# Differential-attention layer: keys stored as two parts in DRAM, their high part read twice

## The chip, the cores and the metric

The kernel runs on one core of a Trainium2 chip. The metric is the device time of one execution in microseconds (us). The core has a matrix engine (PE, TensorE), whose granted clock the profile shows, a vector engine (DVE), a scalar engine (ACT), GpSimd (POOL), and SyncE (SP), which in this kernel issues every transfer (DMA).

## The reference, cut to what matters

One layer of a hybrid encoder is run for 2048 prompt rows and for 64 sample rows that see a cache of 1024 earlier keys. The change touches the product of queries and keys alone:

```python
proj = x @ p['w_in']
q, k, v, u = jnp.split(proj, [ATTN_WIDTH, 2 * ATTN_WIDTH, 3 * ATTN_WIDTH], axis=-1)
q = partial_rope(q.reshape(bsz, seq, 2 * N_HEADS, HALF_DIM), pos)
k = partial_rope(k.reshape(bsz, seq, 2 * N_HEADS, HALF_DIM), pos)
...
s = jnp.einsum('bqhd,bkhd->bhqk', q, k).astype(jnp.float32) * (HALF_DIM ** -0.5)
s = jnp.where(mask[None, None], s, -jnp.inf)
a = jax.nn.softmax(s, axis=-1)
w = (a[:, :, 0] - lam * a[:, :, 1]).astype(v.dtype)
o = jnp.einsum('bhqk,bkhd->bqhd', w, v).astype(jnp.float32)
```

There are 16 maps (8 heads of two), each with 32 dimensions for q and k. The rest of the layer is a state-space branch with a gated unit, an output projection, two layer norms and a feed-forward block of width 4096.

## The kernel before, in words

**High and low parts.** A float32 operand of a product is split into a high part in a shorter format and the low part that is left (`split`, line 127: ACT or another engine rounds, line 130 or 132; DVE or POOL subtracts, line 133). A product then takes three terms: high by high, high by low, low by high. For most products these are three matmuls (`mm3`, lines 136 to 138). For queries and keys a map has only 32 dimensions, so the three terms are stacked along the contraction: 3 x 32 = 96 rows in one matmul (line 515), and 99 with three rows of mask for the causal blocks (line 517).

**Writing queries and keys.** `proj_qk` (line 337) runs over 17 blocks of 128 rows. For each it makes q and k (lines 367 to 371), rotates them, and one block later `pend` calls `transposes` (line 346) once for q and once for k: four PE transposes, a split into the tiles tph (high) and tpl (low), and then the writes to DRAM. The scratch tensors have three slots per dimension (lines 216 to 219). Queries are written as high, low, high: slots 0 and 2 get tph, slot 1 gets tpl. Keys are written as high, high, low: slots 0 and 1 get tph, slot 2 gets tpl. That makes three writes for q and three for k in each block; a write has runs of 128 columns (64 for the sample's keys). `cache_keys` (line 394) does the same for the cached keys, eight tiles of 128 x 512, each written three times to KC (lines 413 to 415).

**Reading them.** `load_maps` (line 444) loads what one head needs: for each of two maps a query tile (tag q, three buffers) and one or two key tiles of up to 1024 columns (tag k, five buffers). A query tile is two transfers: 96 rows of QS, where the dimension and the slot of [512, 3, columns] merge into one row index (line 450), and three mask rows (line 451). A key tile is likewise two: 96 rows (line 456) and three mask rows (line 457). The first matmul of a unit that reads a tile waits for all its transfers. Heads are run in four sets of query blocks (line 1332), 8 heads each, and the third set also has a sample unit per head, which reads KC in tiles of 1024 and 64 columns.

**The order of the work.** All transfers stand in one queue, that of SP, in the order which the build gives them. The build orders the instructions of each engine by a model of their times and by priorities (`schedule_with_timeline_sim`, line 1470; `tc.high_priority`), so the order in one engine's queue isn't that of the source. In the projection of q and k (lines 1276 to 1281) the state-space branch is woven in between; in the attention (lines 1331 to 1368) the gated unit, the output projection and the feed-forward block are. A load of weights (tiles raw) or of a map waits in SP's queue until its buffer is free, and all that stands behind it waits too.

Of the kernel before, what the change touches and what calls it, by code (L numbers as in the profile page):

```python
# [13 lines left out]
F32R = mybir.dt.float32r  # L14
# [8 lines left out]
SEQ = 2048  # L23
DEC = 64
PAST = 1024
NT = SEQ + 2 * DEC
NL = NT // 128
AW = 512
# [85 lines left out]
def build(nc, tc, io, ctx):  # L114
# [8 lines left out]
    def dma(out, in_):  # L123
        f = lambda a: a.bitcast(F32) if a.dtype == F32R else a
        sync.dma_start(out=f(out), in_=f(in_))

    def split(dst_hi, dst_lo, src, hi_eng=None, lo_eng=None):

        if (hi_eng or act) is act:
            act.activation(out=dst_hi, in_=src, func=AF.Copy)  # L130
        else:
            hi_eng.tensor_copy(out=dst_hi, in_=src)  # L132
        (lo_eng or dve).tensor_tensor(out=dst_lo, in0=src, in1=dst_hi.bitcast(F32), op=ALU.subtract)  # L133
# [6 lines left out]
    def tt(e, out, a, b, op):  # L140
        e.tensor_tensor(out=out, in0=a, in1=b, op=op)  # L141
# [70 lines left out]
    def scratch(name, shape, dt=F32):  # L212
        return dr.tile(shape, dt, name=name)


    QS = scratch("s_q", [AW, 3, NT], F32R)
    KS = scratch("s_k", [AW, 3, SEQ], F32R)
    KC = scratch("s_kc", [AW, 3, PAST + DEC], F32R)
    QPARTS, KPARTS = ((0, 2), (1,)), ((0, 1), (2,))
    VS = scratch("s_v", [NH, 128, NL, 2, HD], F32R)  # L220
    VC = scratch("s_vc", [NH, 128, PAST // 128, 2, HD], F32R)
    KMS, QMS = (scratch("s_" + n, [3, 1024], F32R) for n in ("km", "qm"))
# [33 lines left out]
    def load_x(xp, b):  # L256

        n = 256 if b < 8 else 128
        h = xp.tile([128, 8, 256], F32R, tag="xh", name="xh")
        l = xp.tile([128, 8, 256], F32R, tag="xl", name="xl")  # L260
        for q in range(4):
            raw = xp.tile([128, 2, 256], F32, tag="xr", name="xr")
            dma(out=raw[:, :, :n], in_=io["xT"][q * 256:(q + 1) * 256, b * 256:b * 256 + n].rearrange("(k p) n -> p k n", p=128))
            split(h[:, 2 * q:2 * q + 2, :n], l[:, 2 * q:2 * q + 2, :n], raw[:, :, :n], lo_eng=XLO[(b + q) % len(XLO)])
        return h, l
# [71 lines left out]
    def proj_qk(wq, wk, xp, x0, c2):  # L337

        op = c2.enter_context(tc.tile_pool(name="o1", bufs=2, side="right"))
        pm = c2.enter_context(tc.tile_pool(name="pm1", bufs=QB, space=PSUM, side="right"))  # L340
        pt = c2.enter_context(tc.tile_pool(name="pt1", bufs=2, space=PSUM, side="right"))
        cs = op.tile([128, 2, NL, 8], F32, name="cs", bufs=1)
        dma(out=cs[:, 0], in_=io["cos8"])
        dma(out=cs[:, 1], in_=io["sin8"])

        def transposes(src, dst, parts, ncol, c0):
            ps = pt.tile([128, 4, 128], F32, tag="pt", name="pt")
            for c in range(4):
                pe.transpose(out=ps[:, c, :], in_=src[:, c * 128:(c + 1) * 128], identity=ident)
            h = op.tile([128, 4, 128], F32R, tag="tph", name="tph")  # L350
            l = op.tile([128, 4, 128], F32R, tag="tpl", name="tpl")
            split(h, l, ps)
            for t_, js in zip((h, l), parts):
                for j in js:
                    dma(out=dst.rearrange("(c p) j n -> p c j n", p=128)[:, :, j, c0:c0 + ncol], in_=t_[:, :, :ncol])

        xs = [x0]
        pend = None
        for i in range(NL):
            if i % 2 == 0:  # L360
                xh, xl = xs.pop(0)
                if i + 2 < NL:
                    xs.append(load_x(xp, i // 2 + 1))
            ts_ = slice(i % 2 * 128, i % 2 * 128 + 128)
            nrow = 128 if i < 16 else 64
            qk = op.tile([128, 1024], F32, tag="qk", name="qk")
            for cg, (wh, wl) in ((1, wk), (0, wq)):
                ps = pm.tile([128, 512], F32, tag="pm", name="pm")
                for kk in range(8):
                    mm3(ps, xh[:, kk, ts_], xl[:, kk, ts_], wh[:, kk], wl[:, kk], kk == 0, kk == 7)  # L370
                act.activation(out=qk[:, cg * 512:cg * 512 + 512], in_=ps, func=AF.Copy, scale=(SM_SCALE, 1.0)[cg])
            x8 = qk.rearrange("p (m d) -> p m d", d=32)[:, :, 0:8]
            ra = op.tile([128, 32, 8], F32, tag="ra", name="ra", bufs=1)
            rb = op.tile([128, 32, 8], F32, tag="rb", name="rb", bufs=1)
            tt(dve, ra, x8, cs[:, 0, i:i + 1, :].to_broadcast([128, 32, 8]), ALU.mult)
            tt(dve, rb[:, :, 0:4], x8[:, :, 4:8], cs[:, 1, i:i + 1, 0:4].to_broadcast([128, 32, 4]), ALU.mult)
            tt(dve, rb[:, :, 4:8], x8[:, :, 0:4], cs[:, 1, i:i + 1, 4:8].to_broadcast([128, 32, 4]), ALU.mult)
            tt(dve, x8, ra, rb, ALU.add)
            r0 = i * 128
            dma(out=io["k_o"][r0:r0 + nrow, :], in_=qk[:nrow, 512:1024])  # L380
            if pend:
                pend()

            def pend(qk=qk, i=i, r0=r0):
                transposes(qk[:, 0:512], QS, QPARTS, 128, r0)
                if i < 16:
                    transposes(qk[:, 512:1024], KS, KPARTS, 128, r0)
                else:
                    transposes(qk[:, 512:1024], KC, KPARTS, 64, PAST)
            yield  # L390
        pend()
        yield

    def cache_keys(c2):
        op = c2.enter_context(tc.tile_pool(name="ck", bufs=CKB, side="right"))
        for i in range(PAST // 128):
            raw = op.tile([128, 512], F32, tag="ckr", name="cvr")
            dma(out=raw, in_=io["cv"][i * 128:i * 128 + 128, :])
            for q, t_ in enumerate("hl"):
                vv = op.tile([128, 4, 2, HD], F32R, tag="ck" + t_, name="cvv")  # L400
                split_v(vv, raw[:, q * 256:q * 256 + 256])
                dma(out=VC.rearrange("h p i e d -> p i h (e d)")[:, i, q * 4:q * 4 + 4], in_=vv.rearrange("p h e d -> p h (e d)"))
            if i % 2:
                yield
        for c in range(4):
            for hf in range(2):
                h = op.tile([128, 512], F32R, tag="ckh", name="ckh")
                l = op.tile([128, 512], F32R, tag="ckl", name="ckl")
                rr, cc = slice(c * 128, (c + 1) * 128), slice(hf * 512, hf * 512 + 512)
                raw = op.tile([128, 512], F32, tag="ckr", name="ckr")  # L410
                dma(out=raw, in_=io["ckT"][rr, cc])
                split(h, l, raw, hi_eng=pool, lo_eng=pool)
                for t_, js in zip((h, l), KPARTS):
                    for j in js:
                        dma(out=KC[rr, j, cc], in_=t_)
                yield


# [25 lines left out]
    def load_maps(a, h, ksrc, nk, q0, nq):  # L444

        kt, qt = [], []
        for m in range(2):
            r = slice((2 * h + m) * 32, (2 * h + m) * 32 + 32)
            qt.append(a.qp.tile([KROWS, 512], F32R, tag="q", name="qst"))
            dma(out=qt[m][0:96, :nq], in_=QS[r, :, q0:q0 + nq].rearrange("r j n -> (r j) n"))  # L450
            dma(out=qt[m][96:KROWS, :nq], in_=QMS[:, :nq])
            kt.append([])
            for c0 in range(0, nk, 1024):
                n = min(nk - c0, 1024)
                t = a.kp.tile([KROWS, 1024], F32R, tag="k", name="kst") if n > 64 else a.k2.tile([KROWS, 64], F32R, tag="k%d" % m, name="ks2")
                dma(out=t[0:96, :n], in_=ksrc[r, :, c0:c0 + n].rearrange("r j n -> (r j) n"))
                dma(out=t[96:KROWS, :n], in_=KMS[:, :n])
                kt[m].append(t)
        return kt, qt
# [163 lines left out]
    def head_units(a, h, j0, j1):  # L623
        got = []

        def head():
            if not got:
                nk = j1 * 256
                kst, qst = load_maps(a, h, KS, nk, j0 * 256, nk - j0 * 256)
                vt = [a.vp.tile([128, 8, 128], F32R, tag="v", name="vt") for c in range(0, 2 * j1, 8)]  # L630
# [7 lines left out]
    def sample_unit(a, h):  # L638
        got = []

        def head():
            if not got:
                kst, qst = load_maps(a, h, KC, PAST + DEC, SEQ, DEC)
                vt = [a.vp.tile([128, 8, 128], F32R, tag="v", name="vt"), a.k2.tile([128, 1, 128], F32R, tag="v", name="vt2")]
# [715 lines left out]
    with cw:  # L1360
# [13 lines left out]
        with ExitStack() as c2:  # L1374
# [3 lines left out]
            b, l = B[3], B[2]  # L1378
# [23 lines left out]
            t = third()  # L1402
# [82 lines left out]
```

## Time and profile before

| what | value |
|---|---|
| median of 2 runs | 3099.81 us (3096.27 and 3103.34) |
| the profiled execution: its own time | 3108.33 us |
| its span, first to last instruction | 3106.6 us |
| PE busy | 2878.8 us (93% of the span) |
| DVE, ACT, POOL busy | 1768.3, 1501.3, 1646.6 us |
| mean granted clock of PE | 0.955 of full speed |
| bytes moved | 424.41 MB, of them 93.64 MB written to DRAM |

The rows below come from the profiled execution; a busy time of PE counts matmuls in flight, and the granted clock is a share of full speed. The share of DMA is the mean busy share of the core's 16 transfer engines. Transfers that SP issues have no busy time on SP itself; a row of SPq gives how long the issuing instruction stood in SP's sequencer.

### The profile page before, as it was taken

The numbers are of one execution on the slowest core, as the hardware profiler recorded it, in microseconds if no ns is written. First come the engines' busy times: TensorE is split into PE (matmuls) and PEld (weight loads), VectorE is DVE, ScalarE is ACT, GpSimd is POOL, SyncE is SP. The second block draws the span as 40 slices with busy tenths as digits, with TensorE's granted clock in tenths as the row PEclk, the third lists the DMA queues.
The fourth block names the chain that finished last, engine by engine and source line by source line (L and its number), as shares of the span: only waits on it lengthen the run. The fifth ranks groups of instructions, "written<-read, shape, count | busy, mean of one in ns | idle before, by whom it ended". The sixth has DMA issues, their size and how long they took to land.

```text
span 3106.6 us, 46392 instructions
## 1 busy us (share of the span) xinstructions
PE 2878.8 (93%) x15648; PEld 2415.2 (78%) x15648; DVE 1768.3 (57%) x4631; ACT 1501.3 (48%) x2905; POOL 1646.6 (53%) x1552
## 2 busy tenths in 40 slices
PE   8998999698989999999789999998799999989996
PEld 7976666598778888887578888876588888868885
DVE  7126776568787655658687666666526222442124
ACT  4222222677676666766566766752323333323332
POOL 2227752255665656656555666654545444555554
PEclk9999999699889999999889999999899999999998
DMA  6369774756744444446633333337322222253332
GB/s 190 114 202 229 211 193 125 219 156 188 224 131 127 144 120 125 128 133 196 186 110 111 107 107 111 94 112 264 98 83 68 79 82 82 82 170 94 99 99 71
DMA packets 419618, 424.41 MB, mean 137 GB/s; under 512 B 53394, under 2 KB 312978, under 8 KB 418356
## 3 DMA queue, kind: packets, MB, share of 16 engines
q1 hardware_dynamic: 419380, 421.46, 46.0%
q8 instruction: 123, 2.02, 0.3%
q14 instruction: 115, 0.94, 0.1%
HBM read 327.71 MB, written 93.64 MB: 136 GB/s over the span
## 4 chain that ended last, share of the span: by engine, by line
PE 64%; DVE 12%; DMA 11%; POOL 4%; issue 4%; ACT 3%; SPq 1%; DVEq 0%; POOLq 0%; ACTq 0%
PE pu L138 7%; PE pu L136 7%; PE pd L136 7%; PE pu L137 7%; PE pd L138 7%; PE pd L137 7%; PE oT L578 3%; PE tps L562 3%; PE sps L515 3%; DVE acc L141 2%; DMA raw<-in_ln_g 2%; DVE s L518 2%; POOL dl L133 1%; POOL s L141 1%; PE pm L138 1%
## 5 line engine op out<-in xcount | busy, mean ns | idle before, releaser
L133 POOL TENSOR_TENSOR dl<-raw,dh 128x512 fp32r<-128x512 f32 x336 | 438.5, 1316 | 328.0 <-ACT dh L130 294.0
L133 POOL TENSOR_TENSOR fwl<-raw,fwh 128x512 fp32r<-128x512 f32 x256 | 332.6, 1303 | 327.5 <-ACT fwh L130 288.6
L141 POOL TENSOR_TENSOR s<-s 128x512 f32<-128x512 f32 (+3 forms) x344 | 382.3, 1136 | 227.3 <-ACT s L546 209.3
L518 DVE TENSOR_SCALAR_CACHE_REDUCE s<-sps 128x512 f32<-128x512 f32 (+5 forms) x688 | 400.1, 599 | 169.8 <-PE sps L515 94.7
L136 PE MATMUL pu<-bxh,fwh 128*128 128x256 f32 (+2 forms) x1472 | 488.8, 334 | 3.5 <-ACT fwh L130 1.5
L137 PE MATMUL pu<-bxl,fwh 128*128 128x256 f32 (+2 forms) x1472 | 484.9, 331 | 0.0
L138 PE MATMUL pu<-bxh,fwl 128*128 128x256 f32 (+2 forms) x1472 | 482.1, 331 | 1.0 <-POOL fwl L133 0.9
L136 PE MATMUL pd<-dh,hh 128*128 128x512 f32 (+1 forms) x1088 | 430.3, 401 | 23.2 <-DVE acc L1025 8.6
L137 PE MATMUL pd<-dl,hh 128*128 128x512 f32 (+1 forms) x1088 | 429.8, 396 | 0.0
L138 PE MATMUL pd<-dh,hl 128*128 128x512 f32 (+1 forms) x1088 | 417.3, 397 | 3.8 <-POOL hl L133 2.0
L526 ACT ACTIVATE s<-s,nm 128x1024 f32<-128x1024 f32 (+9 forms) x416 | 365.6, 881 | 112.9 <-DVE nm L523 105.1
L130 ACT ACTIVATE dh<-raw 128x512 fp32r<-128x512 f32 x336 | 209.0, 628 | 390.5 <-PE pd L138 152.7
L141 DVE TENSOR_TENSOR acc<-acc,pd 128x512 f32<-128x512 f32 (+1 forms) x384 | 252.8, 681 | 241.9 <-PE pd L138 239.5
L132 DVE CAST hh<-fr 128x256 fp32r<-128x256 f32 (+2 forms) x184 | 106.2, 577 | 375.6 <-ACT fr L1178 375.4
L136 PEld LDWEIGHTS pu<-bxh,fwh 128*128 128x128 f32 x1472 | 279.3, 190 | 33.2 <-ACT fr L1177 3.0
L130 ACT ACTIVATE fwh<-raw 128x512 fp32r<-128x512 f32 x256 | 160.5, 628 | 295.5 <-DMA raw<-in_w_up 149.4
L137 PEld LDWEIGHTS pu<-bxl,fwh 128*128 128x128 f32 x1472 | 279.1, 190 | 25.4
L138 PEld LDWEIGHTS pu<-bxh,fwl 128*128 128x128 f32 x1472 | 276.5, 189 | 27.5 <-POOL fwl L133 2.6
L578 PE MATMUL oT<-w,vt 128*128 128x256 f32 (+3 forms) x1296 | 251.3, 295 | 14.2 <-DVE w L133 9.4
L136 PEld LDWEIGHTS pd<-dh,hh 128*128 128x128 f32 (+1 forms) x1088 | 202.3, 186 | 68.1 <-DVE hh L132 9.9
L515 PE MATMUL sps<-kst,qst 96*128 96x512 f32 (+2 forms) x544 | 219.6, 422 | 35.5 <-DVE s L518 28.7
L578 PEld LDWEIGHTS oT<-w,vt 128*128 128x128 f32 (+1 forms) x1296 | 206.2, 196 | 43.9 <-DVE w L133 16.3
(273 smaller groups left out, 5921.4 us busy)
## 6 DMA issues: line engine op xcount, KB each, us to landing
raw<-in_w_up SPq DMA_DIRECT2D x256, 256.0 KB
raw<-in_w_down SPq DMA_DIRECT2D x256, 256.0 KB
kst<-s_k SPq DMA_DIRECT2D x64, 384.0 KB
raw<-in_w_out SPq DMA_DIRECT2D x80, 256.0 KB
xr<-in_xT SPq DMA_DIRECT2D x64, 256.0 KB
vt<-s_v SPq DMA_DIRECT2D x32, 512.0 KB
qst<-s_q SPq DMA_DIRECT2D x64, 192.0 KB
s_q<-tph SPq DMA_DIRECT2D x34, 256.0 KB
```

The costliest lines, as they stand in the source:

```text
L130: act.activation(out=dst_hi, in_=src, func=AF.Copy)
L132: hi_eng.tensor_copy(out=dst_hi, in_=src)
L133: (lo_eng or dve).tensor_tensor(out=dst_lo, in0=src, in1=dst_hi.bitcast(F32), op=ALU.subtract)
L136: pe.matmul(ps, lhsT=lh, rhs=rh, start=start, stop=False)
L137: pe.matmul(ps, lhsT=lh, rhs=rl, start=False, stop=False)
L138: pe.matmul(ps, lhsT=ll, rhs=rh, start=False, stop=stop)
L141: e.tensor_tensor(out=out, in0=a, in1=b, op=op)
L515: pe.matmul(ps[:nr, :e - c0], lhsT=qst[m][0:96, q], rhs=self.keys(m, 96, c0, e), start=True, stop=True)
L518: dve.tensor_scalar(out=s[:nr, o:o + c1 - c0], in0=ps[:nr, :c1 - c0], scalar1=1.0, scalar2=None, op0=ALU.mult, op1=ALU.max, accum_out=self ...
L526: act.activation(out=x, in_=x, func=AF.Exp, bias=nm, accum_out=self.ls[:nr, m, p:p + 1])
L562: pe.transpose(out=ps[:kr, i * nr:i * nr + nr], in_=self.s[t, 0, k_ * 128 // SC][:nr, o:o + kr], identity=ident[:nr, :nr])
L578: pe.matmul(self.oT[:, t * nr:(t + n) * nr], lhsT=vt[k_ // 8][:kr, k_ % 8, :], rhs=w[:kr, e, i * nr:(i + n) * nr], start=(k_ == 0 and e == ...
```

## The change

The third slot of keys goes. KS and KC hold high and low; a key tile is now three transfers: 64 rows of both parts (slots merged as before), 32 rows of the high part again, and the mask rows. Queries hold high, high in QS and low in a tensor of their own, QL, so that the 96 rows meet the keys' rows in the same three terms: high by high and high by low in the first 64 rows, low by high in the last 32. A query tile is three transfers too. The writes of q stay three per block; those of k become two. The matmuls, their shapes, the splits and the buffers in SBUF stay as they are. The rows of a tile stand in another order along the contraction, the same for q and k.

```diff
--- before.py
+++ after.py
@@ -213,10 +213,9 @@
         return dr.tile(shape, dt, name=name)
 
 
-    QS = scratch("s_q", [AW, 3, NT], F32R)
-    KS = scratch("s_k", [AW, 3, SEQ], F32R)
-    KC = scratch("s_kc", [AW, 3, PAST + DEC], F32R)
-    QPARTS, KPARTS = ((0, 2), (1,)), ((0, 1), (2,))
+    QS, QL = scratch("s_q", [AW, 2, NT], F32R), scratch("s_ql", [AW, 1, NT], F32R)
+    KS = scratch("s_k", [AW, 2, SEQ], F32R)
+    KC = scratch("s_kc", [AW, 2, PAST + DEC], F32R)
     VS = scratch("s_v", [NH, 128, NL, 2, HD], F32R)
     VC = scratch("s_vc", [NH, 128, PAST // 128, 2, HD], F32R)
     KMS, QMS = (scratch("s_" + n, [3, 1024], F32R) for n in ("km", "qm"))
@@ -343,14 +342,14 @@
         dma(out=cs[:, 0], in_=io["cos8"])
         dma(out=cs[:, 1], in_=io["sin8"])
 
-        def transposes(src, dst, parts, ncol, c0):
+        def transposes(src, parts, ncol, c0):
             ps = pt.tile([128, 4, 128], F32, tag="pt", name="pt")
             for c in range(4):
                 pe.transpose(out=ps[:, c, :], in_=src[:, c * 128:(c + 1) * 128], identity=ident)
             h = op.tile([128, 4, 128], F32R, tag="tph", name="tph")
             l = op.tile([128, 4, 128], F32R, tag="tpl", name="tpl")
             split(h, l, ps)
-            for t_, js in zip((h, l), parts):
+            for t_, (dst, js) in zip((h, l), parts):
                 for j in js:
                     dma(out=dst.rearrange("(c p) j n -> p c j n", p=128)[:, :, j, c0:c0 + ncol], in_=t_[:, :, :ncol])
 
@@ -382,11 +381,11 @@
                 pend()
 
             def pend(qk=qk, i=i, r0=r0):
-                transposes(qk[:, 0:512], QS, QPARTS, 128, r0)
+                transposes(qk[:, 0:512], ((QS, (0, 1)), (QL, (0,))), 128, r0)
                 if i < 16:
-                    transposes(qk[:, 512:1024], KS, KPARTS, 128, r0)
+                    transposes(qk[:, 512:1024], ((KS, (0,)), (KS, (1,))), 128, r0)
                 else:
-                    transposes(qk[:, 512:1024], KC, KPARTS, 64, PAST)
+                    transposes(qk[:, 512:1024], ((KC, (0,)), (KC, (1,))), 64, PAST)
             yield
         pend()
         yield
@@ -410,9 +409,8 @@
                 raw = op.tile([128, 512], F32, tag="ckr", name="ckr")
                 dma(out=raw, in_=io["ckT"][rr, cc])
                 split(h, l, raw, hi_eng=pool, lo_eng=pool)
-                for t_, js in zip((h, l), KPARTS):
-                    for j in js:
-                        dma(out=KC[rr, j, cc], in_=t_)
+                for j, t_ in enumerate((h, l)):
+                    dma(out=KC[rr, j, cc], in_=t_)
                 yield
 
 
@@ -447,13 +445,15 @@
         for m in range(2):
             r = slice((2 * h + m) * 32, (2 * h + m) * 32 + 32)
             qt.append(a.qp.tile([KROWS, 512], F32R, tag="q", name="qst"))
-            dma(out=qt[m][0:96, :nq], in_=QS[r, :, q0:q0 + nq].rearrange("r j n -> (r j) n"))
+            dma(out=qt[m][0:64, :nq], in_=QS[r, :, q0:q0 + nq].rearrange("r j n -> (r j) n"))
+            dma(out=qt[m][64:96, :nq], in_=QL[r, 0, q0:q0 + nq])
             dma(out=qt[m][96:KROWS, :nq], in_=QMS[:, :nq])
             kt.append([])
             for c0 in range(0, nk, 1024):
                 n = min(nk - c0, 1024)
                 t = a.kp.tile([KROWS, 1024], F32R, tag="k", name="kst") if n > 64 else a.k2.tile([KROWS, 64], F32R, tag="k%d" % m, name="ks2")
-                dma(out=t[0:96, :n], in_=ksrc[r, :, c0:c0 + n].rearrange("r j n -> (r j) n"))
+                dma(out=t[0:64, :n], in_=ksrc[r, :, c0:c0 + n].rearrange("r j n -> (r j) n"))
+                dma(out=t[64:96, :n], in_=ksrc[r, 0, c0:c0 + n])
                 dma(out=t[96:KROWS, :n], in_=KMS[:, :n])
                 kt[m].append(t)
         return kt, qt
```

## Rows read from the trace of the kernel before

**Rows 1.** Page, part 4: engines' shares of the chain that ended last

```profile
PE 64%; DVE 12%; DMA 11%; POOL 4%; issue 4%; ACT 3%; SPq 1%; DVEq 0%; POOLq 0%; ACTq 0%
```

**Rows 2.** Busy time by stretch: length; PE, PEld, DVE, ACT, POOL; clock; DMA; GB/s

```profile
233.00:544.00 311.00, 284.16 (x1318) 201.18 (x1317) 222.88 (x325) 83.51 (x177) 178.56 (x274) 0.95 0.71 189
544.00:622.00 78.00, 48.80 (x236) 40.71 (x234) 45.90 (x192) 49.06 (x136) 20.83 (x27) 0.67 0.74 220
622.00:785.00 163.00, 153.40 (x1159) 146.01 (x1158) 127.60 (x464) 123.30 (x292) 87.44 (x107) 0.95 0.60 182
785.00:830.00 45.00, 40.44 (x207) 33.17 (x207) 27.60 (x83) 29.00 (x53) 27.77 (x24) 0.92 0.82 255
830.00:1475.00 645.00, 620.89 (x3444) 524.23 (x3442) 445.76 (x1310) 435.97 (x865) 393.36 (x333) 0.98 0.47 137
1475.00:1630.00 155.00, 124.65 (x661) 101.29 (x662) 117.62 (x337) 95.76 (x170) 84.50 (x70) 0.86 0.50 149
1630.00:2042.00 412.00, 404.31 (x2258) 348.15 (x2257) 269.84 (x723) 280.60 (x493) 256.26 (x212) 0.99 0.36 104
2042.00:3106.00 1064.00, 986.28 (x5096) 829.82 (x5094) 419.67 (x871) 335.35 (x591) 537.30 (x432) 0.96 0.35 107
```

**Rows 3.** Issues on SP by tile, whole span: ns minimum/median/maximum, first and last start

```profile
L125 SPq DMA_DIRECT2D s_k<-tph x32: 359/640/1050, 252.1 to 573.4; - x32
...
L125 SPq DMA_DIRECT2D s_kc<-ckh x16: 328/432/1125, 317.4 to 424.8; - x16
...
L125 SPq DMA_DIRECT2D s_kc<-tph x2: 455/652/849, 583.0 to 583.5; - x2
...
L125 SPq DMA_DIRECT2D qst<-s_q x80: 303/319/1190, 544.0 to 1967.7; - x80
...
L125 SPq DMA_DIRECT2D kst<-s_k x96: 303/312/1397, 544.8 to 1971.5; - x96
...
L125 SPq DMA_DIRECT2D kst<-s_kc x16: 303/327/772, 911.5 to 1444.2; - x16
...
L125 SPq DMA_DIRECT2D ks<-s_kc x16: 303/304/314, 596.1 to 1405.5; - x16
```

**Rows 4.** What PE waited for from 235 to 545: us in total, times, longest

```profile
PE pm L136 <- ACT xh L130: 3.5, 1, 3.5
```

**Rows 5.** What PE waited for from 545 to 2042, the loads of maps

```profile
PE sps L517 <- DMA qst<-s_q: 7.8, 1, 7.8
PE sps L517 <- DMA qst<-s_qm: 7.3, 1, 7.3
...
PE sps L515 <- DMA qst<-s_q: 2.6, 2, 2.1
...
PE sps L517 <- DMA kst<-s_k: 1.7, 2, 1.1
```

**Rows 6.** What SP's queue waited for from 622 to 2042

```profile
SPq L125 <- POOL fwl L133: 200.9, 92, 10.2
...
SPq L125 <- DMA raw<-in_w_up: 47.9, 29, 4.3
```

**Rows 7.** Timeline of SP, 553 to 567: start, length, what is issued

```profile
553.04 1.48 SPq L125 DMA_DIRECT2D gyg<-s_gy  x3
...
558.22 0.24 SPq L125 DMA_DIRECT2D qst<-s_qm  x1
561.86 0.30 SPq L125 DMA_DIRECT2D kst<-s_k  x1
565.54 0.56 SPq L125 DMA_DIRECT2D kst<-s_km  x2
```

**Rows 8.** Timeline of SP, 788 to 804

```profile
790.62 0.33 SPq L125 DMA_DIRECT2D qst<-s_q  x1
...
796.07 0.24 SPq L125 DMA_DIRECT2D kst<-s_km  x1
...
803.91 0.38 SPq L125 DMA_DIRECT2D s_o<-o  x1
```

## The prediction

> **What bounds the kernel now.** I began with the chain of work that ended last: PE has 64% of it, DMA 11%, SP's sequencer 1% [rows 1]. So a transfer counts mainly where PE stands still for it. Next came the busy time by stretch [rows 2], cut where the stages change. The reader is to see three kinds of stretch. From 233 to 544 (projection of q and k, where the keys are written) PE is busy for 284.2 of 311 us, and the transfer engines are well used, 0.71 at 189 GB/s. From 544 to 622 (the attention starts, its first maps are loaded) PE is busy for only 48.8 of 78 us and its granted clock is 0.67, a mixture of its two levels, 2.4 and 1.2 GHz. From 622 to 2042 it is 153.4 of 163, 40.4 of 45, 620.9 of 645, 124.7 of 155 and 404.3 of 412. What lies behind 2042 (1064 us) reads no query or key and isn't touched. Then the waits: which idle time of PE a transfer ended, in the writing stage [rows 4] and in the attention [rows 5], what SP's queue waits for [rows 6], and two pieces of its timeline [rows 7, 8].
>
> **Part one, writes that go.** 16 of the 32 writes of tph to the keys, 8 of the 16 of ckh and one of the two of the sample's keys are gone: 25 issues. By their medians they stood on SP for 16 x 0.640 + 8 x 0.432 + 0.652 = 14.3 us [rows 3]. In bytes: tiles of 128 x 512 x 4 are 256 KB, so 24 x 256 KB and 128 KB, 6.4 MB. From 233 to 544 some 311 us x 189 GB/s = 58.8 MB move [rows 2], so the stage loses about a tenth of its traffic. If that traffic set its pace, 6.4 MB at 189 GB/s would give 34 us; PE's idle time there is 311 - 284.2 = 26.8 us, so 27 us is the most that can come back. What PE waited for says it is far less: the one wait that can stand behind a load is that for ACT rounding x, 3.5 us [rows 4]. I take about half of it, -2 us; bounds -27 and 0. It lies at the small end because PE's named wait is the nearest row. The write of q is not less: three issues of the same size before and after, one to another tensor.
>
> **Part two, reads that are split.** Bytes read stay the same: 96 rows, now 64 and 32. The count of issues grows by one for each query tile and each key tile: 80 + 96 + 16 + 16 = 208 [rows 3]. Each stood on SP for 0.30 to 0.33 us by the medians; I take 0.31, 64.5 us of SP's time in all. By the start times of these issues 28 of the 208 fall into 544 to 622, 26 into 622 to 785, 8 into 785 to 830, 106 into 830 to 1475, 12 into 1475 to 1630, and 28 behind it.
>
> There is also a limit on how many transfers are open at once, which the trace of before shows [rows 7]: three loads of 1 MB go out at 553.04, five small issues follow, and the ninth counted from the first, the mask rows at 558.22, comes late; the two after it come 3.6 and 3.7 us apart, at 561.86 and 565.54. I read this as eight places, each free again when its transfer has landed. An extra small transfer thus costs an issue, and in a crowded stretch also a place.
>
> *544 to 622.* The 28 issues are 28 x 0.31 = 8.7 us; two of the removed writes fell here too (one of keys and one of the sample's keys, 0.640 and 0.652), so 7.4 us net on SP. PE stalls here for loads of maps, 7.8 and 7.3 us [rows 5], so nothing hides them but the waits for the big loads, which stay. Part of the issues belong to heads behind the last stall; I take two thirds, +5 us. Bounds: 0 (all behind the 1 MB loads) and 28 x 1.2 = 34 us, if each costs the crowded pace that follows.
>
> *785 to 830.* SP crawls: from 790.62 to 803.91 eleven issues go out, 1.2 us each [rows 8], with the transfer engines at 0.82 [rows 2]. PE waits 2.1 us for a query tile at this place [rows 5], so two more issues in front of that matmul show in full: 2 x 1.2 = +2.5 us. Bounds 0 and 8 x 1.2 = 10.
>
> *The other 172 issues*, 172 x 0.31 = 53 us of SP, lie beside a PE that is nearly always busy. Their cover is SP's own idle time: it waited 200.9 us for POOL to free tiles of weights alone [rows 6], and a queue that waits for a buffer doesn't lose by having issued two small loads before. PE's waits for loads of maps outside the two places above are about 2 us (2.6 less 2.1, and 1.7 for key tiles) [rows 5]. I take +1 us; bounds 0 and, with the cover gone, 53.
>
> **Sum.** -2 + 5 + 2.5 + 1 = +6.5 us, so 3108.3 + 6.5 = 3114.8 us for an execution like the profiled one. That one is 8.5 us above the median of the runs shown, so against the median the forecast is 3099.8 + 6.5 = 3106 us.
>
> **A rule against the change.** Small transfers overlap until the places run out [rows 7, 8]. The Trainium skill, "DMA: Bandwidth & Descriptors", section "Rules for kernel authors", tells to merge many small transfers into one, since under 64 KB mostly overhead is paid; the split-off part of a query tile, 32 x 512 x 4 bytes, is just 64 KB. Its section "Anatomy of one DMA" (for the other issue path) fits a fixed cost of about 2.0 us per DMA; an estimate from that, all in series, is 208 x 2 = 416 us and 3516 us in all. The trace speaks against paying it in series: the two issues at 565.54 take 0.56 us on SP together [rows 7], and the page itself says that the fixed cost overlaps if the DMA is issued early. What is left of the rule is the second rival.
>
> **The rivals.**
> 1. *The writing stage is paced by its transfers.* For it: share 0.71, the highest of the long stretches. Against: PE waits there 3.5 us for anything that stands behind a transfer [rows 4]. All 26.8 us of idle come back in place of 2: 3106 - 25 = 3081 us.
> 2. *Slower: SP's queue becomes the bound of the attention.* The mechanism: a load of weights stands behind extra loads of maps, comes late, and PE's fill runs dry. Each extra issue then costs its 0.31 us in full, 64.5 us, and in 544 to 622 and 785 to 830 the crowded pace instead, 36 x (1.2 - 0.31) = 32 us on top; less the 14.3 us of writes: +82 us, 3182 us, 2.7% more. It decides from the point where SP's waits for freed buffers are used up. For it: 47.9 us of SP's waits from 622 to 2042 are already for earlier loads of weights to land. Against: 200.9 us for one kind of buffer alone [rows 6].
> 3. *Another order.* The build orders the queues by a model of time, and 208 more and 25 fewer transfers change what it sees. How much an unlucky order is worth, one stretch shows: 1475 to 1630 has 30 us of PE idle and a clock of 0.86 beside neighbours at 0.98 and 0.99 [rows 2]. One such stretch more or less: 3136 or 3076 us.
> 4. *The change doesn't relieve anything*, because what is read, by far the larger part, stays the same in bytes. That is so, and stands in the sum already; the result would then be the forecast without its -2.
>
> **How the numbers follow.** Chances: the forecast (with its own range 3095 to 3120, rival 4 in it) 0.57; rival 1 0.10; rival 3 0.25, split evenly; rival 2 0.08. Against the median, faster or slower by over 2% means below 3037.8 or above 3161.8 us, which is about what a measurement of this kernel can tell from no change. Nothing of the kind stands below (the idle time of the whole writing stage is 27 us), so faster gets 0.03 for an order that I can't foresee; slower gets 0.06, most of rival 2; within 2%: 0.91. The range takes in rivals 1 and 3 and not rival 2: 3076 to 3138 us.
>
> **What would show it.** Right: the stretch from 233 to 544 is within 5 us of its length with its DMA share below 0.71; in the stretch that follows, PE's waits for query and key loads sum to some 20 us instead of 15, and PE is idle some 5 us longer; SP's waits for freed buffers shrink by about 50 us from 622 to 2042 and PE's busy share there stays. Wrong: the writing stage is shorter by 15 us or more; or new waits of ACT or PE on loads of weights in the attention sum to tens of us; or the two traces have their stalls in other places, so that the order, not the transfers, made the difference.

## The result: 1.3% slower, and the profile after

| | before | after |
|---|---|---|
| median | 3099.81 us | 3139.40 us (3137.42 and 3141.39) |
| profiled execution: own time, span | 3108.33, 3106.6 us | 3137.42, 3135.2 us |
| PE busy, mean clock | 2878.8 us, 0.955 | 2905.1 us, 0.948 |
| bytes moved, of them written to DRAM | 424.41, 93.64 MB | 418.00, 87.22 MB |

The ratio is 1.0129, 95% interval [1.0095, 1.0164]: 40 us slower, where 6 were forecast. The 6.4 MB of writes are gone as counted.

The shares of the chain that ended last, after, against [rows 1]:

```profile
PE 61%; DMA 13%; DVE 12%; POOL 4%; ACT 4%; issue 3%; SPq 2%; DVEq 0%; POOLq 0%; ACTq 0%
```

PE lost three points; DMA gained two and SP's sequencer one. The stretches of after, against [rows 2], with the same columns:

```profile
233.00:544.00 311.00, 285.60 (x1343) 202.64 (x1343) 224.22 (x337) 86.37 (x184) 175.58 (x273) 0.96 0.66 174
544.00:622.00 78.00, 50.88 (x204) 41.09 (x205) 42.40 (x181) 47.54 (x133) 21.11 (x27) 0.53 0.65 196
...
830.00:1475.00 645.00, 621.10 (x3422) 520.81 (x3422) 428.06 (x1295) 437.20 (x862) 386.90 (x327) 0.97 0.47 135
1475.00:1630.00 155.00, 123.62 (x597) 99.98 (x596) 116.06 (x337) 91.86 (x157) 80.17 (x66) 0.80 0.53 154
...
2042.00:3135.00 1093.00, 1015.40 (x5204) 849.98 (x5202) 424.79 (x875) 341.50 (x600) 551.25 (x443) 0.96 0.35 106
```

No large hole opened: in the first four of these stretches, and in 622 to 785 and 785 to 830, PE is busy for as long as before, within some 2 us; from 1630 to 2042 it is 396.9 us in place of 404.3. What differs more is the count of matmuls in brackets: in the same length 204 where there were 236, then 597 where there were 661, and 1015 us of PE's work are left behind 2042 where 986 were. The last matmul of the attention (tile oT) comes at 2078 us, before at 2080. So the attention keeps pace; what falls behind is the fill, the feed-forward matmuls woven in beside it, and at the end the rest of it is simply longer. A busy share doesn't show this; the counts do. The granted clock fell in the two stretches that lost most matmuls, from 0.67 to 0.53 and from 0.86 to 0.80, so a busy PE got less done there; whether that is a cause or a consequence of the delay, no run here parts.

The issues on SP after, whole span, by tile, against [rows 3]:

```profile
L125 SPq DMA_DIRECT2D kst<-s_k x192: 302/451/1639, 532.5 to 1961.6; - x192
...
L125 SPq DMA_DIRECT2D qst<-s_q x80: 445/451/1721, 530.7 to 1955.3; - x80
L125 SPq DMA_DIRECT2D qst<-s_ql x80: 302/576/1960, 531.2 to 1955.8; - x80
```

Here is the surprise of the case. A 96-row load stood 0.31 to 0.32 us on SP. The 64-row load that takes its place stands 0.45 us, though it moves less, and the 32-row load behind it 0.58 us. A split load costs 1.03 us of SP and not 0.62.

### The profile page after: what moved, and what is told of

It is laid out like the page before. It is cut to its first block, busy times and chain, and to the rows that moved or that the text cites. A ratio compares the mean times of both kernels' runs of the same rounds, so it can differ in the third digit from the quotient of the medians.

```text
span 3135.2 us, 46637 instructions
## 1 busy us (share of the span) xinstructions
PE 2905.1 (93%) x15648; PEld 2428.5 (77%) x15648; DVE 1743.5 (56%) x4631; ACT 1507.6 (48%) x2905; POOL 1642.6 (52%) x1552
## 2 busy tenths in 40 slices
DMA packets 412818, 418.00 MB, mean 133 GB/s; under 512 B 55810, under 2 KB 307202, under 8 KB 411556
## 3 DMA queue, kind: packets, MB, share of 16 engines
HBM read 327.71 MB, written 87.22 MB: 132 GB/s over the span
## 4 chain that ended last, share of the span: by engine, by line
PE 61%; DMA 13%; DVE 12%; POOL 4%; ACT 4%; issue 3%; SPq 2%; DVEq 0%; POOLq 0%; ACTq 0%
PE pd L136 7%; PE pd L137 7%; PE pu L136 7%; PE pu L138 7%; PE pd L138 7%; PE pu L137 7%; PE oT L578 3%; PE tps L562 3%; PE sps L515 3%; DMA raw<-in_w_up 2%; DVE acc L141 2%; SPq L125 2%; DMA raw<-in_ln_g 2%; DVE s L518 2%; DMA raw<-in_w_out 1%
## 5 line engine op out<-in xcount | busy, mean ns | idle before, releaser
L578 PE MATMUL oT<-w,vt 128*128 128x256 f32 (+3 forms) x1296 | 256.5, 302 | 28.4 <-ACT w L130 18.1
```

The lines of the kernel that those rows point to most:

```text
L578: pe.matmul(self.oT[:, t * nr:(t + n) * nr], lhsT=vt[k_ // 8][:kr, k_ % 8, :], rhs=w[:kr, e, i * nr:(i + n) * nr], start=(k_ == 0 and e == ...
```

## The experiments

The build orders each engine's queue anew for every kernel, so transfers and order change together. To part them, most kernels below are held in the order of before: each instruction is tied, without a semaphore, to the one that is to stand ahead of it on its engine (an added transfer stands right behind its neighbour). All 15,648 matmuls of two traces then pair one to one, and the start of one less that of its partner is an offset that can be followed through the kernel.

```diff
+    for a, b in zip(row, row[1:]):
+        tc.add_manual_dep(b, a.name, no_sync, reason="order")
```

The ties themselves change nothing: built with its own order tied, the kernel before has the same instructions on every engine. All ratios are to the kernel before in the same group of runs. "SP" is the time of all issues on SP from 520 to 2045 us, added up over the rows of the trace.

| run | order | SP, us | ratio [95%] |
|---|---|---|---|
| before | own | 402 | 1 |
| e2 before's transfers | of after | 396 | 1.0032 [1.0020, 1.0045] |
| e3 split 64+32 | own | 549 | 1.0091 [1.0074, 1.0108] |
| e4 writes removed | own | 388 | 1.0031 [1.0016, 1.0045] |
| e7, e15 writes removed | of before | 394, 398 | 0.9962 [0.9944, 0.9979], 0.9963 [0.9948, 0.9978] |
| e10 96 rows, long issue | of before | 461 | 1.0014 [0.9996, 1.0031] |
| e6 split 48+48 | of before | 491 | 1.0037 [1.0020, 1.0055] |
| e12 writes removed, 48+48 | of before | 492 | 1.0023 [1.0009, 1.0037] |
| e5, e14 split 64+32 | of before | 543, 547 | 1.0094 [1.0076, 1.0112], 1.0103 [1.0083, 1.0123] |
| e1, e11 whole change | of before | 543, 540 | 1.0098 [1.0080, 1.0117], 1.0102 [1.0081, 1.0123] |
| e13 writes removed, 64+32 | of before | 543 | 1.0098 [1.0077, 1.0119] |
| e9 48+48, long issue | of before | 555 | 1.0083 [1.0063, 1.0103] |
| e8 split 32+32+32 | of before | 579 | 1.0145 [1.0127, 1.0164] |
| e16 whole change, masks on ACT | of before | 480 | 1.0109 [1.0083, 1.0135] |
| e17 before, masks on ACT | of before | 343 | 1.0071 [1.0053, 1.0089] |

**Order or transfers (e1 to e4).** e1 has the transfers of after in the order of before, e2 the reverse. e3 splits the reads alone; e4 removes the writes alone, with one 96-row read that runs on into the next map's rows:

```diff
-    KS = scratch("s_k", [AW, 3, SEQ], F32R)
+    KS = scratch("s_k", [AW, 2, SEQ], F32R)
...
+                r0 = min(2 * r.start, 2 * AW - 96)
-                dma(out=t[0:96, :n], in_=ksrc[r, :, c0:c0 + n].rearrange("r j n -> (r j) n"))
+                dma(out=t[0:96, :n], in_=ksrc[:, :, c0:c0 + n].rearrange("r j n -> (r j) n")[r0:r0 + 96])
```

> The transfers of the changed kernel, with every engine's instructions (SP's queue too) held in the order that the kernel before has; an added read stands right behind the read it was split from. Nothing of the computation is changed. Theory O (the 40 us come from the order that the build chose once the transfers differed): 3095 to 3108 us, that is within some 8 us of the kernel before. Theory T (the 40 us are what 208 more issues cost on SP and in open places): 3132 to 3145 us, like the changed kernel. In between, say 3115 to 3125, both have a share.

> The counterpart: the transfers of the kernel before (96 rows in one read, keys written three times), with every engine's instructions held in the order that the changed kernel has. Theory O: 3128 to 3145 us, as slow as the changed kernel though not one transfer is added. Theory T: 3094 to 3106 us, like the kernel before.

> Half of the change: three slots and three writes of keys as before, but each read of 96 rows is issued as 64 and 32 rows (208 more issues); the build chooses its own order. Theory T: at least 3139 us, since it has all the issues and not the 25 writes that went, so 3140 to 3155. Theory O: its order is a third draw, so anywhere from 3075 to 3140 us, and the time should not sit at the changed kernel's but by accident.

> The other half: keys stored as high and low, 25 writes less, but each key tile is still read by one transfer of 96 rows in a row of the two-slot tensor, so the last 32 rows belong to the next map and the products of queries and keys are other numbers; no issue is added. The build chooses its own order. Theory T: 3085 to 3100 us, never slower than the kernel before. Theory O: a fourth draw, anywhere from 3075 to 3140 us; slower than 3106 us would speak against T outright.

e1 keeps most of the loss (+0.98% of 1.29%), e2 shows a quarter of it (+0.32%). So the transfers come first and the order second. e3 points at the reads, though its 3123.7 us lie below the 3140 to 3155 expected for that case. e4 is slower than before although it only leaves work out, which is possible only through its own order, as e7 then showed.

**Which property of a read costs (e5 to e8).** In the order of before: the reads split as 64 and 32 (e5), as 48 and 48 (e6), in three of 32 (e8), and the writes removed alone (e7).

```diff
-            dma(out=qt[m][0:96, :nq], in_=QS[r, :, q0:q0 + nq].rearrange("r j n -> (r j) n"))
+            src = QS[r, :, q0:q0 + nq].rearrange("r j n -> (r j) n")
+            dma(out=qt[m][0:48, :nq], in_=src[0:48])
+            dma(out=qt[m][48:96, :nq], in_=src[48:96])
```

> Three slots and all writes as before; each read of 96 rows is issued as 64 and 32 rows; every engine held in the order of the kernel before. This is the price of the split reads alone. The first run (all of the change in the old order) came out 34 us over the kernel before with a writing stage some 16 to 19 us shorter. So both theories below expect 40 to 55 us over the kernel before; under 25 us would mean that the loss isn't in the reads.

> As the run with 64 and 32 rows, but each read is split into 48 and 48 rows: the same 208 more issues, the same bytes, the same order. Theory S (SP's time by shape: in the traces a 64-row issue stands 0.45 us and the 32-row one behind it 0.57 us, against 0.31 us for 96 rows, so a split read costs 0.7 us more and not 0.31): with two issues of 0.31 us the loss is under half of that of 64 and 32, 10 to 22 us over the kernel before. Theory N (each transfer takes one of eight open places, whatever its shape): the same loss as with 64 and 32 rows, within 8 us.

> Keys stored twice, 25 writes less, each key tile read by one transfer of 96 rows in a row of the two-slot tensor (so the last 32 rows are the next map's, and the products of queries and keys are other numbers); every engine in the order of the kernel before. The gain of the writes alone: 10 to 20 us under the kernel before if what the first run showed in the writing stage (16 to 19 us shorter) lasts to the end; 0 to 5 us under it if the start of the attention gives it back.

> As the run with 64 and 32 rows, but each read is split into three of 32 rows: 416 more issues, the order as before. Theory N: twice the loss of 64 and 32, 80 to 110 us over the kernel before. Theory S: three issues of some 0.31 us take as much of SP as 0.45 and 0.57 us do, so about the same loss as 64 and 32, 35 to 60 us.

e5 and e6 have the same number of transfers, the same bytes and the same order, and e6 loses 0.37% where e5 loses 0.94% (some 29 us, where 40 to 55 were expected). So the number of transfers can't be the whole price. The issues on SP differ: 0.31 and 0.42 us by the medians for the two halves of e6 (sorted by their place in the pair), 0.45 and 0.58 for e5. e8 has twice the added transfers of e5, but all of the short kind (0.31, 0.42, 0.42), and loses half as much again, not twice as much. From here on theory S says that SP's issue time is the price, theory N that the number of transfers is.

**The same transfers, another issue (e9, e10).** In the built programs an issue carries a mark when it was prepared ahead; the loads of maps of 32, 48 and 96 rows carry it, those of 64 don't. e9 is e6 with the mark taken off the first of each pair; e10 is the kernel before with it taken off its 96-row loads.

```diff
+    def long_way(out, in_):
+        nc.dge_precook = False
+        dma(out=out, in_=in_)
+        nc.dge_precook = True
...
-            dma(out=qt[m][0:48, :nq], in_=src[0:48])
+            long_way(out=qt[m][0:48, :nq], in_=src[0:48])
```

> The transfers of e6 (each map load of 96 rows as 48 and 48, three writes, the order of before), with one thing changed: the first 48-row transfer of each pair is built without the short form of issue that it has in e6, as the 64-row transfers of e5 were. No byte, no transfer and no wait differs from e6. Theory S (the loss is the time that SP stands on its issues): the pair goes from about 0.73 us of SP to about 1.03, SP's extra time from 95 towards 148 us, and the loss from the 0.37% of e6 to the 0.94% of e5: 1.007 to 1.010. Theory N (the loss is the number of transfers, or of what they keep open at the DMA engines): as e6, 1.003 to 1.005.

> The kernel before with its own transfers and its own order, and only the 208 map loads of 96 rows built without the short form of issue. No transfer is added. Theory S: a load stands about 0.45 us on SP in place of 0.31 and the mask load behind it up to 0.58 in place of 0.30, together 30 to 90 us more of SP; by the loss that e6 showed at 95 us (+11.5 us) that gives 0 to +11 us, 1.000 to 1.004. Theory N: no change, 0.999 to 1.001. If the time of a long issue is not on SP but at the DMA engines (packets smaller or more of them), the DMA share rises and SP's issue times don't.

The key loads on SP in e6, then in e9, then in e10 with the mask load behind it:

```profile
L129 SPq DMA_DIRECT2D kst<-s_k x192: 302/413/2170, 528.2 to 1968.0; - x192
```

```profile
L134 SPq DMA_DIRECT2D kst<-s_k x192: 302/556/1952, 529.5 to 1988.7; - x192
```

```profile
L134 SPq DMA_DIRECT2D kst<-s_km x112: 238/456/525, 527.3 to 1963.8; - x112
L134 SPq DMA_DIRECT2D kst<-s_k x96: 488/495/1004, 526.6 to 1963.3; - x96
```

e9 is the run that decides. Only the form of 208 issues differs from e6, the DMA packets (422,949 and 422,948) and the mean DMA share (0.48 from 520 to 2045) are alike, SP's time rises from 491 to 555 us, and the loss goes from 0.37 to 0.83%, nearly that of e5; the two intervals don't overlap. e10 shows both halves of the price without any added transfer: 0.50 us for the load itself, and 0.46 in place of 0.30 us for the mask load behind it. SP stands 59 us longer from 520 to 2045, and this costs 0.14% at the most likely, which can't be told from nothing. If SP's time alone is the price, the first 60 us or so are covered, the next 30 (e6) cost about 11 us in all, and by 140 to 150 us (e5, e14) some 30 are lost.

What the number of transfers adds by itself stays open. e6 adds 208 transfers and 89 us of issue time together, and e8, with 208 transfers more than e9 and only 24 us more on SP, loses 0.62% more. In what SP waits for it doesn't show. The eight open places of the prediction and of theory N are a wait of this program: as built, SP's transfers take eight semaphores in turn, and each may start only when the one issued eight before it has landed. SP's waits for landings from 622 to 2042 sum to 108 us before, 99 in e6, 95 in e9 and 99 in e8, so they didn't grow.

**Do the halves add (e11 to e15)?** e1 lost more than e5 and e7 together, so they were repeated side by side, with two kernels between them: the writes removed and the reads split, but reading on into the next map's rows instead of back to the high rows (e13), and the same with 48 and 48 (e12).

```diff
-                dma(out=t[0:64, :n], in_=ksrc[r, :, c0:c0 + n].rearrange("r j n -> (r j) n"))
-                dma(out=t[64:96, :n], in_=ksrc[r, 0, c0:c0 + n])
+                src = ksrc[:, :, c0:c0 + n].rearrange("r j n -> (r j) n")[r0:r0 + 96]
+                dma(out=t[0:64, :n], in_=src[0:64])
+                dma(out=t[64:96, :n], in_=src[64:96])
```

> The kernel of e1 once more, unchanged, with more rounds: there the whole change cost 0.98%, while its two halves apart gave -0.38% (e7) and +0.94% (e5), +0.56% by their sum. If the halves add, and e1 was an upper stray, 1.004 to 1.007. If the two halves really work on each other, 1.009 to 1.011 again.

> Both halves of the change in the order of before, but with the map loads cut as 48 and 48 rows and not as 64 and 32: keys in two slots and written twice (e7), and every map load in two transfers of 48 rows (e6). The keys' loads run on into the next map's rows, so the third key row of each dimension is another one than the reference's. Theory S, and halves that add: -0.38% + 0.37%, 0.998 to 1.002, with SP's extra time for the map loads at about 95 us less 14 for the writes. Theory N, or halves that work on each other as in e1: 1.004 to 1.010.

> As e12 (keys in two slots, written twice, order of before, loads running on into the next map's rows so that the third key row is another one), but cut as 64 and 32 rows. It is e11 with one difference: the second key read does not go back to the high rows of its own map, it reads on. If reading the high rows twice costs something of its own: 1.004 to 1.007, below e11's 1.0102. If only the cut as 64 and 32 and SP's time for it count (theory S): as e11, 1.008 to 1.012.

> The kernel of e5 once more: three writes, loads cut as 64 and 32, order of before. Beside e13 and e15 on one chip it tells whether the halves of the change add. If they add: about 0.4% above e13. If the gain of the removed writes is lost once SP is the bound of the attention (theory S): within 0.2% of e13, 1.008 to 1.011.

> The kernel of e7 once more: two writes, one 96-row load that reads on into the next map's rows, order of before. 0.995 to 0.998 if e7 stands; 0.999 or more if e7 was a lower stray, and then the halves add after all with nothing gained by the removed writes.

All repeats stand. Removing the writes gains 0.37% when the reads are whole (e15), nothing that can be seen with 48 and 48 (e12 against e6: 1.0023 and 1.0037, the intervals overlap), and nothing with 64 and 32 (e13 against e14). Reading the high rows twice costs nothing that can be seen (e13 against e11, which also differ in how queries are stored). So the halves don't add (e12 lies just above the 0.998 to 1.002 expected if they did); that the gain is used up once SP is late fits theory S, but no run shows how.

**Relief (e16, e17).** The 208 mask loads (0.30 us each) are issued by ACT and not by SP: in the whole change (e16) and in the kernel before (e17).

```diff
-                dma(out=t[96:KROWS, :n], in_=KMS[:, :n])
+                nc.scalar.dma_start(out=g(t[96:KROWS, :n]), in_=g(KMS[:, :n]))
```

> The kernel of e11 (the whole change in the order of before), with the 208 mask loads of three rows that stand behind the map loads (0.30 us each on SP, 61 us in all) issued by ScalarE's queue and not by SP. Every transfer stays, in number and size. Theory S: SP's issue time between 520 and 2045 us falls from 540 to about 480 us, the level of e6 and e12, and the loss from 1.0% to about 0.3%: 1.001 to 1.006, if what ScalarE then waits for freed buffers costs little; at the worst ScalarE stands behind those waits and the gain is lost, which ScalarE's own idle time before the mask loads would show. Theory N (the number of transfers): 1.009 to 1.012.

> The kernel before with its own transfers and its own order, and only the 208 mask loads issued by ScalarE's queue and not by SP, as in e16. It tells what that move costs by itself, so that e16 can be read. If ScalarE pays for it, standing in its order behind the waits for freed buffers that SP stood behind (theory S, with a cost of the move that hid the relief): 1.004 to 1.009, and e16 less this run is the 0.1 to 0.6% that theory S leaves at SP's 480 us. If the move costs nothing: 0.997 to 1.002; then e16's loss is not SP's time, and theory S is wrong or incomplete.

e16 alone looks like a defeat of theory S: SP has 60 us less to do and the loss stays, in the range expected for theory N. e17 gives a reason: the move costs 0.71% by itself. ACT now stands in its order behind the waits for freed buffers, and behind landings: of some 48 us that it stood idle ahead of mask loads in e17, 19 ended with a matmul of queries and keys (sps), and 26 with the landing of a transfer that the mask doesn't read (gyg from s_gy 9 us, bxl from s_mxl 7, acc from in_xn 5). Its timeline in e17 (start, length, what; idle before in brackets):

```profile
1538.13 0.58 ACT L139 ACTIVATE w<-tps 128x512 fp32r<-128x512 f32 x1
1543.11 0.25 ACTq L127 DMA_DIRECT2D kst<-s_km  x1
1543.73 1.15 ACT L539 ACTIVATE s<-s,nm 128x1024 f32<-128x1024 f32 x1 [5.02 <-DVE rs_u L150]
```

Between the end at 1538.71 and the mask load at 1543.11 ACT stands 4.4 us behind one issue. Against e17 the split reads of e16 cost 1.0109/1.0071, 0.38% (about 0.3% either way, from the two intervals), where with the masks on SP they cost 1.02% (e11). That fits the relief that theory S asks for, paid for on another engine, if the costs of the move and of the reads add; e16 itself is no faster than e11, so a relief isn't shown. The Trainium skill, "DMA: Bandwidth & Descriptors", section "Issuing engines are not separate DMA queues", says that issuing from several engines saves only the sequencer's time, usually small beside the transfer. Here it was not small in effect: 64 us more of it, with the same transfers, cost 0.46% from e6 to e9, and saving 59 us of it on SP (402 to 343) by issuing on ACT made the kernel 22 us slower.

**How SP's time may reach PE.** What ACT waited for from 622 to 2042, loads of weights alone (us in total, times, longest); first before:

```profile
ACT fwh L130 <- DMA raw<-in_w_up: 53.6, 36, 3.4
ACT dh L130 <- DMA raw<-in_w_down: 22.2, 23, 3.3
ACT dh L130 <- DMA raw<-in_w_out: 18.3, 13, 5.7
```

The whole change in the order of before (e11):

```profile
ACT fwh L134 <- DMA raw<-in_w_up: 67.4, 37, 4.9
ACT dh L134 <- DMA raw<-in_w_down: 35.4, 28, 3.8
ACT dh L134 <- DMA raw<-in_w_out: 24.6, 11, 7.6
```

And with the masks moved off SP (e16):

```profile
ACT fwh L139 <- DMA raw<-in_w_up: 49.2, 35, 3.4
ACT dh L139 <- DMA raw<-in_w_out: 22.5, 11, 6.8
ACT dh L139 <- DMA raw<-in_w_down: 21.9, 21, 3.2
```

94 us, then 127, then 94 again. Of the other held runs with split reads, the sums are 104 (e6), 116 (e9), 118 and 123 (e5, e14) and 123 us (e8), so ACT waits longer for weights when SP is loaded. But this sum doesn't follow the loss: e10 has 115 and loses nothing that can be told, e16 has 94 and loses 1.09%, and e3, in its own order, has 66 and loses 0.91%.

A count on SP follows it better: the loads of weights that go out within 0.15 us of the transfer ahead, so that SP didn't stand idle before them. From 622 to 2042 these are 83 of 287 before, 91 of 288 in e10, 107 of 287 in e6, 115 of 285 in e9, 114 to 117 of 280 to 285 in the five held runs with 64 and 32 and all masks on SP, and 120 of 278 in e8; in its own order after has 94 of 278. More loads of weights thus find SP busy ahead of them. That this is the way on which the loss reaches PE is argued, not shown.

Why SP's idle time would not help, its timeline suggests. One burst of map loads, before:

```profile
1051.02 0.50 SPq L125 DMA_DIRECT2D kst<-s_k  x1
1051.62 0.38 SPq L125 DMA_DIRECT2D qst<-s_q  x1
1052.04 0.30 SPq L125 DMA_DIRECT2D qst<-s_qm  x1
1052.38 0.27 SPq L125 DMA_DIRECT2D kst<-s_km  x1
1052.70 0.31 SPq L125 DMA_DIRECT2D kst<-s_k  x1
1053.05 0.29 SPq L125 DMA_DIRECT2D kst<-s_km  x1
1056.14 0.36 SPq L125 DMA_DIRECT2D raw<-in_w_down  x1
```

The same burst in e11:

```profile
1049.40 1.09 SPq L129 DMA_DIRECT2D kst<-s_k  x2
1050.58 0.45 SPq L129 DMA_DIRECT2D qst<-s_q  x1
1051.09 0.57 SPq L129 DMA_DIRECT2D qst<-s_ql  x1
...
1052.36 1.08 SPq L129 DMA_DIRECT2D kst<-s_k  x2
1053.49 0.29 SPq L129 DMA_DIRECT2D kst<-s_km  x1
1054.04 0.36 SPq L129 DMA_DIRECT2D raw<-in_w_down  x1
```

Map loads go out in bursts. This one took 2.3 us (1051.02 to 1053.34) and now takes 4.4 (1049.40 to 1053.78). Behind it stands a load of weights that had 2.8 us of slack and has 0.26. Here the slack just suffices. A longer burst, or one with less idle time behind it, would push the weights back. This also fits the shape of the table: a first part that costs little, then more for each us.

**Where it is lost.** Growth of the offset in us between the same matmuls, by the marks of before's own trace (544, 622, 830, 1630, end):

| | 544-622 | 622-830 | 830-1630 | 1630-end |
|---|---|---|---|---|
| e15 writes removed | -3 | -1 | +6 | -6 |
| e10 long issue, nothing added | -1 | +3 | +9 | +1 |
| e6 48+48 | +1 | +2 | +12 | -5 |
| e14 64+32 | +9 | +4 | +21 | +2 |
| e9 48+48, long issue | +9 | +2 | +21 | 0 |
| e11 whole change | +6 | +5 | +31 | +3 |
| e8 32+32+32 | +14 | +4 | +34 | 0 |

All rows are measured against the one profiled execution of before, and what was particular to it stands in every row alike: e15, which only leaves writes out, shows +6 from 830 to 1630. Most of the loss falls there, and most of that before 1475 (23 of e11's 31 us), where the attention runs beside a nearly full PE. From 830 to 1475 SP's issues rose from 170 us (458 of them) to 235 (540) in e11.

No version that computes the reference's product was found to beat the kernel before: e7 and e15 are faster, but need a single 96-row read to fetch the high rows twice from two slots.

## Why the prediction was wrong, step by step

- **What bounds the kernel**: PE with its woven fill, and transfers only where PE stands still. Too narrow. In e11 PE's waits from 622 to 2042 sum to 99.0 us, before to 73.4, and no group of them grew by more than 4.4 us (oT for w of ACT, from 3.7 to 8.1). PE is late in many small pieces, and few of them name a transfer.
- **Removed writes, -2 us in the writing stage**: not contradicted. Held in the order of before, seven runs with two writes reach 544 us at offsets of -19.0 to -20.6 (mean -19.7), seven with three at -16.4 to -21.1 (mean -18.1), so the difference is smaller than the spread. That all fourteen are 16 to 21 us ahead of the trace of before is a loss of about 16 us between 356 and 501 in that one profiled execution, which no other run in this order shows (601 matmuls in that piece, 684 in e14): part of the idle time that made the bound, and rival 1, was an accident of one execution, and a writing stage shorter by 15 us, a sign of being wrong, says nothing here. But the writes were worth more by themselves, 0.37% or 11 us (e15). About 3 of the rest appear from 544 to 622, where the last of them stood; the remainder isn't placed.
- **The price of an added read, 0.31 us: the term that was mis-sized.** It was taken from the 96-row loads of [rows 3], as if the number of issues mattered and not their form. Measured, the map loads' and masks' issues took 285.0 us in e5 against 136.6 us before: 148 us for 208 reads, 0.71 each, where 64.5 in all were taken.
- **544 to 622, +5 us**: the runs with 64+32 show +6 to +9. Right in size, but not for the reason given: PE's waits for map loads from 545 to 2042 did not rise by 5 us, in after they fell:

```profile
PE sps L517 <- DMA qst<-s_ql: 2.2, 1, 2.2
PE sps L517 <- DMA qst<-s_qm: 1.9, 1, 1.9
PE sps L517 <- DMA kst<-s_k: 1.2, 1, 1.2
PE sps L515 <- DMA qst<-s_q: 0.5, 1, 0.5
```

  against 19.4 us in [rows 5]. The stretch holds fewer matmuls at a clock of 0.53 instead of 0.67; what lowered the clock, no run here parts from the rest.
- **785 to 830, +2.5 us**: measured -2 to +1 in e5, e11, e13 and e14. Not there.
- **"The other 172 issues", +1 us: the step that failed.** "A queue that waits for a buffer doesn't lose by having issued two small loads before" took one wait for a sum of waits. The sign that was asked for did come. What SP waited for after, from 622 to 2042:

```profile
SPq L125 <- POOL fwl L133: 158.1, 83, 6.3
...
SPq L125 <- DMA raw<-in_w_up: 45.8, 23, 3.8
```

  The wait for POOL shrank from the 200.9 us of [rows 6] by 43, near the 50 forecast, and yet a sign of being wrong came beside it: ACT's waits for weights grew by 20 us in after and by 33 in e11. In place of +1 us the runs with 64 and 32 lost 21 to 31 us from 830 to 1630, within the bound of 53; and e9 against e6 shows that issue time on SP is paid for although SP idles: 64 us more of it cost 0.46%. The reading that fits is that idle time in a queue worked in order is usable only where it lies: behind a burst, ahead of the next urgent load.
- **Rival 2**, SP's queue as the bound of the attention, is the mechanism that the runs speak for: e9 shows that SP's issue time counts; that it counts through late weights is argued. It got a chance of 0.08 and a price of +82 us, each issue in full. The transfers cost 1.0% in the old order, 31 us.
- **Rival 3, the order**: e2 gives +0.32%, 10 us, not 30. e4 against e7 is 0.7%, e3 against e5 nothing. That fits the 8 us that remain between after (1.0129) and e11 (1.0102), though these two intervals overlap. What the prediction asked for as a sign of order, stalls in other places, didn't come: PE's idle time lies in the same stretches (27.1 us from 544 to 622 and 31.4 from 1475 to 1630, before 29.2 and 30.4).
- **The range** ended at 3138 us, 1.4 us short. It left rival 2 out; with its mechanism at half price, +41 us, it would have held.

## What to carry to other kernels

Price an added transfer by the issue time of its own form, and where no row shows that form, bound it by the dearest neighbour and not by the one it replaces. Compare it with the slack behind each burst of the queue, not with the queue's idle time in all. When a change alters transfers, hold the old order once: the order alone was worth up to 0.7% here, as much as the thing under study.

## What was not expected of the hardware

- A load of 64 rows stood 0.45 us on SP, one of 96, 48 or 32 rows as the first of its tile 0.31, whatever its size. Taking the mark off made 96 rows 0.50 and 48 rows 0.49.
- The second issue of a tile pays too: 0.42 us behind a short one (e6), 0.58 behind a long one (e5, e9, e11); a mask load 0.30 behind a short load and 0.46 behind a long one (e10). Why the next issue pays, and why the 64-row loads lack the mark, stays open.
